# Sample attention of a hybrid decoder step: key tiles of a step made first, then mask, four logits matmuls and the value matmuls in chains

## The chip, the cores and the metric

One core of a Trainium2 chip runs the kernel. The metric is the device time of one launch in microseconds (us); the kernel before has a median of 2633.11 us over 3 runs (2631.79 to 2635.52).

## What is computed

The kernel is one inference step of a decoder layer: half an FFN, a mixer, half an FFN and a last norm, on 256 prompt rows and 64 sample rows (8 sequences of 8 new tokens). The mixer has a sparse attention (8 query heads, 2 key heads of 128) and a state-space part. The change lies in the attention of the sample rows over a paged cache of 2048 past keys for each sequence:

```python
score = jnp.where(admissible[None], score, -jnp.inf)
_, idx = lax.top_k(score, top)                       # 256 keys per query
k_sel, v_sel = gather_kv(idx)                        # pages of the cache
logits = jnp.einsum('bqkgd,bqskd->bqkgs', qg, k_sel) * HEAD_DIM ** -0.5
logits = jnp.where(valid, logits + bias, -jnp.inf)
p = jax.nn.softmax(logits, axis=-1)
out = jnp.einsum('bqkgs,bqskd->bqkgd', p, v_sel)
```

The kernel doesn't gather keys. It computes the logits of all 2112 keys and adds a mask of a large negative number where a key was not selected.

## The kernel before

Weights stream through SBUF in chunks of 512 KB (`chunk`, L147): a DMA fills `raw`, ScalarE rounds it to `hi` (L152), VectorE makes `lo = raw - hi` (L153), and TensorE takes three matmuls of 320 columns for each 128x128 piece (`mm3`, L163 to L165). Nearly all of TensorE's time is such matmuls.

The order of the instructions on each engine is made by a scheduler from the program's data dependencies and a cost model of its own. Only SP's queue is in the order in which the program is written, in the stage of the change (`manual_schedule(engines={SPE})`). TensorE takes its instructions strictly in the order made. So the matmuls of the sample attention stand among those of projections that have nothing to do with it (the input projection, `project`, and until about 1275 us the heads of the prompt attention), wherever the scheduler thought that their inputs would be there.

The sample attention works on pairs of sequences, i = 0 to 3, and on blocks of 512 keys, kb = 0 to 3: 16 steps. `logits_part(i, kb)` makes one step's logits:

- for each sequence of the pair, `kn` takes four pages of keys (four DMAs of 128 KB on SP, two buffers); eight transposes on TensorE (L136, `pe_t`) put the two key heads into two PSUM tiles, and ScalarE (L1072) and VectorE (L1070) copy these to two tiles `kt`. A step has four `kt`, q = 0 to 3, one for each sequence and key head;
- four logits matmuls (L1076) multiply the 32 query columns of `qS` with one `kt` each. The 32 columns of q go to the PSUM partitions 32q to 32q+31 of one tile `lg`, so each matmul uses 32 of the array's 128 columns, and the four use different ones;
- the mask is a matmul of `Rep` with `mkS` (L1077), over all 128 columns, into the same `lg`; then ScalarE copies `lg` to `pr` (L1078). The step with kb = 3 has a second, short group for the 64 new keys (L1084, L1085), and then the softmax.

`sample_pT` transposes the probabilities of a pair (17 transposes). `out_part(i - 1, kb)` multiplies them with the values one pair later: for each sequence, `vn` takes four pages of values (four buffers; the first sequence's pages by an indirect DMA of POOL, L1120, the second's by DMAs of SP, L1118; for i = 3 both by SP); then 16 matmuls (L1124), four pages by q = 0 to 3, again 32 columns each, q by q in different columns, all into one PSUM tile `po`. With kb = 3 come four more (L1129) for the new keys. The loop at the end of the stage calls `logits_part(i, kb)` and then `out_part(i - 1, kb)`.

A matmul of f32 data by f32 weights is two instructions in the trace, so the 64 logits matmuls appear as 128 and the 256 value matmuls as 512. Transposes and the matmuls of L163 to L165 are one each.

Of the kernel before, what the change touches and what calls it, by code (L numbers as in the profile page):

```python
# [10 lines left out]
F32 = mybir.dt.float32  # L11
# [10 lines left out]
P = 128  # L22
D = 2048
KT = D // P
TP = 256
NB = 8
NS = 8
TS = NB * NS
# [60 lines left out]
def tile_kernel(tc, I, O, ffn=True):  # L89
# [14 lines left out]
    def nm(s):  # L104
        uid[0] += 1
        return f"{s}_{uid[0]}"
# [7 lines left out]
    def pa_():  # L114
        return psA.tile([P, 512], F32, tag="a", name=nm("pa"))

    flip = [0]
# [297 lines left out]

    # ------------------------------------------------------------------ mixer
    Wi = I["w_in"][0]
# [96 lines left out]

    # ---- indexer
    qp = tc.alloc_tile_pool(name="qp", bufs=1)
# [52 lines left out]

    # dt, decays  # L570
    def sm(tag):
# [245 lines left out]

    # ---- prompt attention
    for h in range(NH):
# [33 lines left out]

    # ---- SSD
    cn = pa.tile([P, 12, 27], F32, tag="cn", name="cn", bufs=1)
# [194 lines left out]

    # ---- sample attention
    cv = I["cache_v"][0].rearrange("n k v d -> (n k) (v d)")
# [4 lines left out]

    def logits_part(i, kb, pr_, mx):
        kts = []
        for bb in range(2):  # L1060
            kn = sa.tile([P, 4, 256], F32, tag="kn", name=nm("kn"), bufs=2)
            for g, src in enumerate(pages(I["cache_k"], 2 * i + bb, 4 * kb, 4)):
                SY.dma_start(kn[:, g, :], src)
            for kv in range(2):
                pt = pa_()
                for g in range(4):
                    pe_t(pt[:, g * P:(g + 1) * P], kn[:, g, kv * P:(kv + 1) * P])
                kt = sa.tile([P, 512], F32, tag="kt", name=nm("kt"), bufs=4)
                if kv:
                    V.tensor_copy(kt, pt)  # L1070
                else:
                    S.copy(kt, pt)  # L1072
                kts.append(kt)
        lg = pa_()
        for q in range(4):
            TE.matmul(lg[32 * q:32 * q + 32], qs(i, q), kts[q], start=True, stop=False)  # L1076
        TE.matmul(lg, Rep[:, kb // 2, i, :], mkS[:, 512 * (kb % 2):512 * (kb % 2) + 512], start=False, stop=True)  # L1077
        S.copy(pr_[:, 512 * kb:512 * kb + 512], lg)  # L1078
        if kb < 3:
            V.tensor_reduce(mx[:, kb:kb + 1], pr_[:, 512 * kb:512 * kb + 512], axis=AX.X, op=ALU.max)  # L1080
            return
        lg = pa_()
        for q in range(4):
            TE.matmul(lg[32 * q:32 * q + 32, :TS], qs(i, q), kT[:, q % 2, TP:T], start=True, stop=False)  # L1084
        TE.matmul(lg[:, :TS], Rep[:, 1, i, :], mkS[:, PAST // 2:HK], start=False, stop=True)  # L1085
# [6 lines left out]
        V.tensor_scalar(pr_, pr_, mx[:, 6:7], None, op0=ALU.mult)  # L1092

    def sample_pT(pr_):
# [14 lines left out]

    def out_part(i, kb, pT, po):  # L1110
        vns = []
        for bb in range(2):
            vn = sa.tile([P, 4, 256], F32, tag="vn", name=nm("vn"), bufs=4)
            on_sp = pages(I["cache_v"], 2 * i + bb, 4 * kb, 4) if bb or i == 3 else None
            for g in range(4):
                pg_i = (2 * i + bb) * NPG + 4 * kb + g
                if on_sp is not None:
                    SY.dma_start(vn[:, g, :], on_sp[g])  # L1118
                else:
                    G.indirect_dma_start(out=vn[:, g, :], out_offset=None, in_=cv, in_offset=bass.IndirectOffsetOnAxis(ap=pti[:, pg_i:pg_i + 1], axis=0))  # L1120
            vns.append(vn)
        for g in range(4):
            for q in range(4):
                TE.matmul(po[32 * q:32 * q + 32, :P], pT[:, 4 * kb + g, 32 * q:32 * q + 32], vns[q // 2][:, g, (q % 2) * P:(q % 2 + 1) * P],  # L1124
                          start=(kb == 0 and g == 0), stop=False)
        if kb < 3:
            return
        for q in range(4):
            TE.matmul(po[32 * q:32 * q + 32, :P], pT[:TS, 16, 32 * q:32 * q + 32], vnat[:TS, 2, (q % 2) * P:(q % 2 + 1) * P], start=False, stop=True)  # L1129
        osb = sa.tile([P, 512], F32, tag="kt", name=nm("osb"), bufs=4)[:, 0:P]  # L1130
        S.copy(osb, po[:, :P])
# [7 lines left out]
    for i in range(5):  # L1139
# [65 lines left out]

    # ---- output projection
    Wo = I["w_out"][0]
# [105 lines left out]
```

## Time and profile before

| what | value |
|---|---|
| median of 3 runs | 2633.11 us (2631.79 to 2635.52) |
| span of the profiled execution (the page gives no other time of it) | 2630.1 us |
| TensorE busy, share of the span | 2581.9 us, 98% |
| chain that ended last: share of TensorE | 89% |
| mean granted TensorE clock | 0.994 |
| stage of the sample attention, first logits matmul to the point where both orders are the same again | 1221.8 to 1468.0 us |
| in that stage: DMA engines' busy share, bytes per second | 0.65, 197 GB/s |
| in that stage: VectorE and ScalarE busy | 112.6 and 105.0 of 246.2 us |

How to read it: a page gives one execution by the hardware's profiler. PE is TensorE's matmuls, PEld its weight loads, DVE is VectorE, ACT ScalarE, POOL GpSimd, and SPq the queue of SyncE, which issues most DMAs. In a timeline row, the first number is the start and the second the duration; consecutive matmuls of one form are one row with their count behind x. Matmuls are pipelined: one that has just started lets the next start before its end, so what a matmul costs is the distance from its start to the start of the next, and not its duration. Matmuls in different columns of the array can run beside each other, and their rows then overlap.

### The profile page before, as it was taken

What the parts mean: (1) busy time and instruction counts of PE and PEld (TensorE: products, weight loads), DVE (VectorE), ACT (ScalarE), POOL (GpSimd) and SP (SyncE); (2) the same over time, 40 slices, a digit from 0 to 9 for tenths busy, and PEclk for the clock granted to TensorE, in tenths of its full rate; (3) what the DMA queues carried; (4) which work ended last, traced back from release to release, by engine and by line L of the source; (5) the groups of instructions that cost most, each with busy time, mean ns of one, the idle gap of its engine ahead of it and who ended that gap; (6) DMA issues with size and microseconds to landing.
All of it is one profiled execution on the core that took longest, in us unless ns stands there. A gap on an engine that the chain in (4) does not pass through costs nothing.

```text
span 2630.1 us, 43071 instructions
## 1 busy us (share of the span) xinstructions
PE 2581.9 (98%) x17617; PEld 2446.9 (93%) x17617; DVE 1333.8 (51%) x2052; ACT 1042.2 (40%) x1446; POOL 180.4 (7%) x243
## 2 busy tenths in 40 slices
PE   8999999999999999999999999999999999999997
PEld 7999999999999998787676878999999999999997
DVE  6444444444444556686444466644444444444444
ACT  5333333333333443675443444533333333333333
POOL 3000000000000020000331121200000000000001
PEclk9999999999999999999999999999999999999999
DMA  6444444444454454245666544444444444444443
GB/s 204 145 146 151 152 147 150 153 148 150 142 159 148 156 165 144 76 122 170 186 198 210 174 141 151 137 150 148 152 152 146 152 152 146 151 144 155 151 137 120
DMA packets 401282, 399.70 MB, mean 152 GB/s; under 512 B 22344, under 2 KB 395949, under 8 KB 400572
## 3 DMA queue, kind: packets, MB, share of 16 engines
q1 hardware_dynamic: 366380, 358.76, 44.0%
q10 hardware_dynamic: 30800, 26.23, 3.4%
q0 software_dynamic: 3904, 11.96, 1.4%
q8 instruction: 138, 2.26, 0.3%
q14 instruction: 60, 0.49, 0.1%
HBM read 386.00 MB, written 10.88 MB: 151 GB/s over the span
## 4 chain that ended last, share of the span: by engine, by line
PE 89%; DVE 4%; DMA 2%; ACT 1%; issue 1%; SPq 0%; POOL 0%; ACTq 0%; DVEq 0%; POOLq 0%
PE pw L164 10%; PE pw L163 10%; PE pw L165 9%; PE pa L164 9%; PE pa L163 9%; PE pa L165 9%; PE pm L163 9%; PE pm L164 9%; PE pm L165 9%; PE pa L1076 2%; PE pa L136 1%; DVE lo L153 1%; PE pm L136 1%; PE pm L1124 1%; PE pa L677 1%
## 5 line engine op out<-in xcount | busy, mean ns | idle before, releaser
L153 DVE TENSOR_TENSOR lo<-raw,hi 128x1024 fp32r<-128x1024 f32 (+1 forms) x659 | 798.1, 1213 | 882.6 <-ACT hi L152 873.8
L152 ACT CAST hi<-raw 128x1024 fp32r<-128x1024 f32 (+1 forms) x659 | 676.1, 1026 | 1084.1 <-PE pm L164 439.7
L163 PE MATMUL pw<-xh,hi 128*128 128x320 f32 x1360 | 427.0, 314 | 3.7 <-ACT hi L152 1.7
L165 PE MATMUL pw<-xh,lo 128*128 128x320 f32 x1360 | 424.8, 312 | 2.3 <-DVE lo L153 2.3
L164 PE MATMUL pw<-xl,hi 128*128 128x320 f32 x1360 | 425.2, 313 | 0.7 <-DVE xl L188 0.7
L163 PE MATMUL pa<-xh,hi 128*128 128x320 f32 x1056 | 326.5, 309 | 0.3 <-ACT hi L152 0.3
L165 PE MATMUL pa<-xh,lo 128*128 128x320 f32 x1056 | 326.2, 309 | 0.0
L165 PE MATMUL pm<-xh,lo 128*128 128x320 f32 x1056 | 326.2, 309 | 0.0
L164 PE MATMUL pa<-xl,hi 128*128 128x320 f32 x1056 | 326.1, 309 | 0.0
L163 PE MATMUL pm<-xh,hi 128*128 128x320 f32 x1056 | 325.9, 309 | 0.0
L164 PE MATMUL pm<-xl,hi 128*128 128x320 f32 x1056 | 325.8, 308 | 0.0
L163 PEld LDWEIGHTS pw<-xh,hi 128*128 128x128 f32 x1360 | 256.6, 189 | 12.8 <-issue 10.4
L165 PEld LDWEIGHTS pw<-xh,lo 128*128 128x128 f32 x1360 | 256.2, 188 | 12.0 <-issue 9.3
L164 PEld LDWEIGHTS pw<-xl,hi 128*128 128x128 f32 x1360 | 256.3, 188 | 10.9 <-issue 9.3
L163 PEld LDWEIGHTS pa<-xh,hi 128*128 128x128 f32 x1056 | 198.6, 188 | 0.7 <-ACT hi L152 0.4
L165 PEld LDWEIGHTS pa<-xh,lo 128*128 128x128 f32 x1056 | 198.6, 188 | 0.2
L165 PEld LDWEIGHTS pm<-xh,lo 128*128 128x128 f32 x1056 | 198.5, 188 | 0.3
L164 PEld LDWEIGHTS pa<-xl,hi 128*128 128x128 f32 x1056 | 198.6, 188 | 0.1
L163 PEld LDWEIGHTS pm<-xh,hi 128*128 128x128 f32 x1056 | 198.5, 188 | 0.1
L164 PEld LDWEIGHTS pm<-xl,hi 128*128 128x128 f32 x1056 | 198.5, 188 | 0.0
L197 POOL TENSOR_TENSOR acc<-acc,sq 128x320 f32<-128x320 f32 x55 | 60.3, 1096 | 1864.7 <-ACT sq L195 1863.8
L163 PE MATMUL pm<-hh,hi 128*128 128x320 f32 x528 | 162.9, 308 | 0.0
(445 smaller groups left out, 4014.2 us busy)
## 6 DMA issues: line engine op xcount, KB each, us to landing
raw<-in_w_ffn_dram SPq DMA_DIRECT2D x511, 512.0 KB
raw<-in_w_in_dram SPq DMA_DIRECT2D x40, 512.0 KB
raw<-in_w_in_dram ACTq DMA_DIRECT2D x40, 512.0 KB
kn<-in_cache_k_dram SPq DMA_DIRECT2D x128, 128.0 KB
raw<-in_w_out_dram SPq DMA_DIRECT2D x32, 512.0 KB
vn<-in_cache_v_dram SPq DMA_DIRECT2D x80, 128.0 KB
raw<-in_w_ffn_dram SPq DMA_DIRECT2D x34, 256.0 KB
hn<-in_state_ssm_dram SPq DMA_DIRECT2D x16, 256.0 KB
```

Source lines behind the costliest of these rows:

```text
L136: TE.transpose(out, in_, cst[:n, C_ID:C_ID + n])
L152: S.copy(hi, raw)
L153: V.tensor_sub(lo, raw, hi.bitcast(F32))
L163: TE.matmul(out, wh, xh, start=start, stop=False)
L164: TE.matmul(out, wh, xl, start=False, stop=False)
L165: TE.matmul(out, wl, xh, start=False, stop=stop)
L197: (V if k == KT - 1 else G).tensor_add(accs[0], accs[0], sq)
L677: TE.matmul(pr[:, bh * 256:(bh + 1) * 256], qq[:, b].rearrange("p h t -> p (h t)"), kk[:, :, :, b * NPG:(b + 1) * NPG], start=st, stop=not st)
L1076: TE.matmul(lg[32 * q:32 * q + 32], qs(i, q), kts[q], start=True, stop=False)
L1124: TE.matmul(po[32 * q:32 * q + 32, :P], pT[:, 4 * kb + g, 32 * q:32 * q + 32], vns[q // 2][:, g, (q % 2) * P:(q % 2 + 1) * P], start=(kb = ...
```

## The change

- `logits_part` is cut in two. `load_k` loads the pages and makes all four `kt` of the step; the new `logits_part` gets them. The loop calls `load_k(i, kb)`, `load_v(i - 1, kb)` (the loads of the former `out_part`), then `logits_part`, then `out_part`.
- The mask matmul comes first in its PSUM group (`start=True`) and the four logits matmuls after it (`start=False, stop=True`).
- A new helper, `block`, adds dependencies by hand: the first of the four logits matmuls depends on all four copies to `kt`, and each of the four on the one before it. The same for the value matmuls: the first of 16 (20 with kb = 3) depends on all eight loads of the step's pages, each on the one before it, and the first also on the last logits matmul of the step. The dependencies between matmuls set only the order on TensorE; those on copies and loads are waits.
- The pool of `kt` has 5 buffers in place of 4.

Ten lines are added above the stage, so L136 becomes L146, L163 to L165 become L173 to L175, L1076 becomes L1086, L1077 L1085, L1084 L1094, L1124 L1136, L1129 L1139.

```diff
+    def block(mms, inputs):
+        for m in inputs:
+            tc.add_manual_dep(mms[0].ins, m.ins.name, SYNC, reason="block inputs")
+        for a, b in zip(mms, mms[1:]):
+            tc.add_manual_dep(b.ins, a.ins.name, NOSYNC, reason="block order")
...
-                kt = sa.tile([P, 512], F32, tag="kt", name=nm("kt"), bufs=4)
-                if kv:
-                    V.tensor_copy(kt, pt)
-                else:
-                    S.copy(kt, pt)
+                kt = sa.tile([P, 512], F32, tag="kt", name=nm("kt"), bufs=5)
+                made.append(V.tensor_copy(kt, pt) if kv else S.copy(kt, pt))
                 kts.append(kt)
+        return kts, made
+
+    def logits_part(i, kb, pr_, mx, kts, made):
         lg = pa_()
-        for q in range(4):
-            TE.matmul(lg[32 * q:32 * q + 32], qs(i, q), kts[q], start=True, stop=False)
-        TE.matmul(lg, Rep[:, kb // 2, i, :], mkS[:, 512 * (kb % 2):512 * (kb % 2) + 512], start=False, stop=True)
+        TE.matmul(lg, Rep[:, kb // 2, i, :], mkS[:, 512 * (kb % 2):512 * (kb % 2) + 512], start=True, stop=False)
+        mms = [TE.matmul(lg[32 * q:32 * q + 32], qs(i, q), kts[q], start=False, stop=True) for q in range(4)]
+        block(mms, made)
...
-    def out_part(i, kb, pT, po):
-        vns = []
+    def load_v(i, kb):
+        vns, made = [], []
...
+    def out_part(i, kb, pT, po, vns, made, before):
+        mms = [TE.matmul(po[32 * q:32 * q + 32, :P], pT[:, 4 * kb + g, 32 * q:32 * q + 32], vns[q // 2][:, g, (q % 2) * P:(q % 2 + 1) * P],
+                         start=(kb == 0 and g == 0), stop=False) for g in range(4) for q in range(4)]
...
+        block(mms, made)
+        if before:
+            block(before[-1:] + mms[:1], [])
...
         for kb in range(4):
+            mms = None
             if i < 4:
-                logits_part(i, kb, pr_, mx)
+                kts, made = load_k(i, kb)
             if i > 0:
-                out_part(i - 1, kb, pT, po)
+                vns, vmade = load_v(i - 1, kb)
+            if i < 4:
+                mms = logits_part(i, kb, pr_, mx, kts, made)
+            if i > 0:
+                out_part(i - 1, kb, pT, po, vns, vmade, mms)
```

How this moves TensorE's instructions, at three places. In the rows, L163 to L165 (L173 to L175) are matmuls of a projection, `pa_` and `pm_` are PSUM tiles, and the number behind a tile's name tells one buffer from another.

TensorE before, the step i = 1, kb = 2, the four logits matmuls of `pa_12296`:

```order
L1076 MATMUL pa_12296<-kt_12259,qS 32x512
L136 MATMUL pa_12282<-cst,kn_12268 128x128 x2
L136 MATMUL pa_12289<-cst,kn_12268 128x128 x2
L1076 MATMUL pa_12296<-kt_12266,qS 32x512
L165 MATMUL pw_13875<-xh_8346,lo_13969 128x320
L163 MATMUL pw_14024<-xh_8345,hi_14028 128x320
L164 MATMUL pw_14024<-xl_8347,hi_14028 128x320
L1076 MATMUL pa_12296<-kt_12287,qS 32x512
```

The same step after the change:

```order
L173 MATMUL pw_14025<-xh_8345,hi_14058 128x320
L1086 MATMUL pa_12315<-kt_12259,qS 32x512
L1086 MATMUL pa_12315<-kt_12266,qS 32x512
L1086 MATMUL pa_12315<-kt_12287,qS 32x512
L1086 MATMUL pa_12315<-kt_12294,qS 32x512
L174 MATMUL pw_14025<-xl_8347,hi_14058 128x320
```

Before, each of the four stands alone between matmuls that use all 128 columns; after, the four stand in a row, and the mask's matmul has moved ahead of them.

TensorE before, value matmuls of the same step:

```order
L1124 MATMUL pm_12041<-vn_12309,pT_12011 32x128 x2
L1124 MATMUL pm_12041<-vn_12304,pT_12011 32x128 x2
L163 MATMUL pw_14024<-xh_8345,hi_14028 128x320
L1124 MATMUL pm_12041<-vn_12309,pT_12011 32x128 x2
L1124 MATMUL pm_12041<-vn_12304,pT_12011 32x128 x2
L164 MATMUL pw_14024<-xl_8347,hi_14028 128x320
```

And after:

```order
L175 MATMUL pw_14024<-xh_8346,lo_14089 128x320
L1136 MATMUL pm_12041<-vn_12296,pT_12011 32x128 x2
L1136 MATMUL pm_12041<-vn_12301,pT_12011 32x128 x2
...
L1136 MATMUL pm_12041<-vn_12296,pT_12011 32x128 x2
L1136 MATMUL pm_12041<-vn_12301,pT_12011 32x128 x2
L173 MATMUL pw_14024<-xh_8346,hi_14088 128x320
```

Before, a page's four value matmuls stand together, with a projection's matmul between pages; after, all 16 stand in a row.

TensorE after, the step i = 2, kb = 0: the last transposes of the first key buffer (`kn_12491`) and the first of the load that takes its place (`kn_12590`):

```order
L146 MATMUL pa_12512<-cst,kn_12491 128x128 x4
L146 MATMUL pa_12533<-cst,kn_12519 128x128 x4
L146 MATMUL pa_12540<-cst,kn_12519 128x128 x4
L1085 LDWEIGHTS Rep
L1085 MATMUL pa_12566<-mkS,Rep 128x512
L174 MATMUL pw_14175<-xl_8347,hi_14208 128x320
...
L174 MATMUL pw_14174<-xl_8348,hi_14238 128x320
L146 MATMUL pa_12604<-cst,kn_12590 128x128
L1086 MATMUL pa_12566<-kt_12510,qS 32x512
```

Between the two stand eight transposes, the mask and eight projection matmuls; a transpose of the new load stands ahead of the step's logits.

Over the whole stage, TensorE's order before has the 352 matmuls of 32 columns (64 + 16 of logits, 256 + 16 of values) in 101 unbroken runs; after, the same matmuls stand in 30 runs. The runs that hold logits matmuls of 512 keys are 48 before and 18 after; those that hold value matmuls are 53 and 16. Before, 60 runs are followed by a projection's matmul; after, 19. SP's order differs only in where three loads of the prompt attention stand. POOL keeps its instructions, some gathers of values a few places earlier or later; ScalarE has two loads of a function table more (32 for 30).

## Rows read from the trace of the kernel before

**Rows 1.** The page: busy time by engine, and the chain that ended last

```profile
PE 2581.9 (98%) x17617; PEld 2446.9 (93%) x17617; DVE 1333.8 (51%) x2052; ACT 1042.2 (40%) x1446; POOL 180.4 (7%) x243
...
PE 89%; DVE 4%; DMA 2%; ACT 1%; issue 1%; SPq 0%; POOL 0%; ACTq 0%; DVEq 0%; POOLq 0%
```

**Rows 2.** Windows: length, busy PE, PEld, DVE, ACT, POOL, clock, DMA share, GB/s

```profile
1441.50:1443.90 2.40, 0.35 (x5) 0.12 (x4) 0.00 (x0) 0.44 (x2) 2.04 (x4) 1.00 0.89 284
1443.90:1447.40 3.50, 3.50 (x17) 2.90 (x18) 0.00 (x0) 0.00 (x0) 0.08 (x1) 0.51 0.80 244
...
1221.80:1468.00 246.20, 241.63 (x1789) 166.59 (x1789) 112.61 (x192) 105.00 (x178) 59.58 (x88) 0.99 0.65 197
```

**Rows 3.** Timeline of PE, a logits matmul alone between others

```profile
1224.83 0.31 PE L163 MATMUL pw<-xh,hi 128*128 128x320 f32 x1
1224.98 0.30 PE L164 MATMUL pw<-xl,hi 128*128 128x320 f32 x1
1225.21 1.04 PE L1076 MATMUL pa<-kt,qS 128*32 128x512 f32 x2
1226.19 0.33 PE L136 MATMUL pa<-cst,kn 128*128 128x128 f32 x1
```

**Rows 4.** Timeline of PE, two, three and four logits matmuls in a row

```profile
1221.84 1.05 PE L1076 MATMUL pa<-kt,qS 128*32 128x512 f32 x4
1222.82 0.41 PE L165 MATMUL pw<-xh,lo 128*128 128x320 f32 x1
...
1244.08 1.06 PE L1076 MATMUL pa<-kt,qS 128*32 128x512 f32 x6
1245.07 0.39 PE L1077 MATMUL pa<-mkS,Rep 128*128 128x512 bf16 x1
...
1273.15 1.90 PE L1076 MATMUL pa<-kt,qS 128*32 128x512 f32 x8
1274.99 0.39 PE L1077 MATMUL pa<-mkS,Rep 128*128 128x512 bf16 x1
```

**Rows 5.** Timeline of PE, value matmuls of one page, and of eight

```profile
1285.24 0.43 PE L1124 MATMUL pm<-vn,pT 128*32 128x128 f32 x8
1285.60 0.42 PE L163 MATMUL pw<-xh,hi 128*128 128x320 f32 x1
1285.85 0.31 PE L164 MATMUL pw<-xl,hi 128*128 128x320 f32 x1
...
1438.67 1.96 PE L1124 MATMUL pm<-vn,pT 128*32 128x128 f32 x64
1440.55 0.84 PE L136 MATMUL pm<-cst,cn 128*27 128x128 f32 x6
```

**Rows 6.** Instructions of tiles kt and vn: count, duration ns min/median/max, first and last start

```profile
L1072 ACT COPY kt<-pa x32: 572/586/611, 1218.1 to 1419.8; 128x512 f32<-128x512 f32 x32
L1070 DVE COPY kt<-pa x32: 681/691/692, 1220.0 to 1420.0; 128x512 f32<-128x512 f32 x32
...
L1120 POOL DMA_INDIRECT vn<-in_cache_v_dram,pti x48: 942/949/1992, 1211.1 to 1409.8; - x48
...
DMA to landing us min/median/max: 4.6/4.9/5.9
```

**Rows 7.** Timeline of PE, key transposes of two loads of one buffer

```profile
1325.55 1.53 PE L136 MATMUL pa<-cst,kn 128*128 128x128 f32 x12
...
1329.94 0.66 PE L136 MATMUL pa<-cst,kn 128*128 128x128 f32 x4
```

**Rows 8.** Chain of waits from 1244 to 1250 us, a load of keys

```profile
1244.59 5.02 DMA kn<-in_cache_k_dram
```

**Rows 9.** Who PE waited for, 1220 to 1480 us: total, times, longest

```profile
PE pm L1124 <- DMA vn<-in_cache_v_dram: 2.0, 1, 2.0
PE pa L136 <- DMA kn<-in_cache_k_dram: 2.0, 2, 1.7
PE pa L136 <- issue: 0.4, 1, 0.4
PE pa L136 <- DVE pr L1092: 0.2, 1, 0.2
```

**Rows 10.** Who SP's queue waited for, 1220 to 1470 us

```profile
SPq L1063 <- PE pa L136: 36.2, 11, 10.1
SPq L1063 <- DMA raw<-in_w_in_dram: 20.9, 7, 5.6
SPq L1118 <- DMA raw<-in_w_in_dram: 13.8, 3, 5.8
```

More of the change, by code (lines that the diff above doesn't have):

```diff
@@ L115, in pa_ @@
         return psA.tile([P, 512], F32, tag="a", name=nm("pa"))
+    SYNC = mybir.DependencyInfo(mybir.DependencyClass.Sync, mybir.DependencyReason.DATA)
+    NOSYNC = mybir.DependencyInfo(mybir.DependencyClass.NoSync, mybir.DependencyReason.DATA)
+    def block(mms, inputs):
[3 more added lines that the diff above has]
+            tc.add_manual_dep(b.ins, a.ins.name, NOSYNC, reason="block order")
     flip = [0]
@@ L1056, in qs, with load_k @@
         return qS[:, 2 * i + q // 2, 4 * (q % 2):4 * (q % 2) + 4, :].rearrange("p g t -> p (g t)")
-    def logits_part(i, kb, pr_, mx):
-        kts = []
+    def load_k(i, kb):
+        kts, made = [], []
         for bb in range(2):
@@ L1080, in logits_part @@
             V.tensor_reduce(mx[:, kb:kb + 1], pr_[:, 512 * kb:512 * kb + 512], axis=AX.X, op=ALU.max)
-            return
+            return mms
         lg = pa_()
-        for q in range(4):
-            TE.matmul(lg[32 * q:32 * q + 32, :TS], qs(i, q), kT[:, q % 2, TP:T], start=True, stop=False)
-        TE.matmul(lg[:, :TS], Rep[:, 1, i, :], mkS[:, PAST // 2:HK], start=False, stop=True)
+        TE.matmul(lg[:, :TS], Rep[:, 1, i, :], mkS[:, PAST // 2:HK], start=True, stop=False)
+        last = [TE.matmul(lg[32 * q:32 * q + 32, :TS], qs(i, q), kT[:, q % 2, TP:T], start=False, stop=True) for q in range(4)]
+        block(mms[-1:] + last, [])
         S.copy(pr_[:, PAST:SK], lg[:, :TS])
@@ L1092, in logits_part @@
         V.tensor_scalar(pr_, pr_, mx[:, 6:7], None, op0=ALU.mult)
+        return mms + last
     def sample_pT(pr_):
@@ L1117, in out_part @@
                 if on_sp is not None:
-                    SY.dma_start(vn[:, g, :], on_sp[g])
+                    made.append(SY.dma_start(vn[:, g, :], on_sp[g]))
                 else:
-                    G.indirect_dma_start(out=vn[:, g, :], out_offset=None, in_=cv, in_offset=bass.IndirectOffsetOnAxis(ap=pti[:, pg_i:pg_i + 1], axis=0))
+                    made.append(G.indirect_dma_start(out=vn[:, g, :], out_offset=None, in_=cv, in_offset=bass.IndirectOffsetOnAxis(ap=pti[:, pg_i:pg_i + 1], axis=0)))
             vns.append(vn)
[L1122 to L1125, printed above, removed]
+        return vns, made
+    def out_part(i, kb, pT, po, vns, made, before):
+        mms = [TE.matmul(po[32 * q:32 * q + 32, :P], pT[:, 4 * kb + g, 32 * q:32 * q + 32], vns[q // 2][:, g, (q % 2) * P:(q % 2 + 1) * P],
+                         start=(kb == 0 and g == 0), stop=False) for g in range(4) for q in range(4)]
+        if kb == 3:
+            mms += [TE.matmul(po[32 * q:32 * q + 32, :P], pT[:TS, 16, 32 * q:32 * q + 32], vnat[:TS, 2, (q % 2) * P:(q % 2 + 1) * P],
+                              start=False, stop=True) for q in range(4)]
+        block(mms, made)
+        if before:
+            block(before[-1:] + mms[:1], [])
         if kb < 3:
             return
-        for q in range(4):
-            TE.matmul(po[32 * q:32 * q + 32, :P], pT[:TS, 16, 32 * q:32 * q + 32], vnat[:TS, 2, (q % 2) * P:(q % 2 + 1) * P], start=False, stop=True)
-        osb = sa.tile([P, 512], F32, tag="kt", name=nm("osb"), bufs=4)[:, 0:P]
+        osb = sa.tile([P, 512], F32, tag="kt", name=nm("osb"), bufs=5)[:, 0:P]
         S.copy(osb, po[:, :P])
```

## The prediction

> **What bounds the kernel now.** I read the page first: TensorE is busy for 98% of the span and makes 89% of the chain that ended last [rows 1]. So what counts is how long TensorE takes for its instructions in their order; work of another engine counts only where TensorE waits for it. The windows come next: from the first logits matmul to the point where both orders are the same again the stage takes 246 us, at full clock but for one piece, with DMA engines 65% busy and VectorE and ScalarE under half [rows 2]. The list of waits says that TensorE stands still in the stage for under 5 us in all: once 2.0 us for a page of values, twice for keys (2.0 us), and two short ones [rows 9]. So the stage is bound by TensorE's stream, and its price is read from the timeline, as distances from start to start.
>
> The timeline shows what the change is about. A projection's matmul is followed by the next after 0.15 us. A logits matmul alone (two records, 32 of 128 columns) holds the stream for 0.98 us, 1225.21 to 1226.19, and starts 0.23 us after its forerunner, not 0.15 [rows 3]. Two in a row take 0.98 us as well, and three 0.99: they run beside each other in their own columns [rows 4]. Four in a row are in the trace too, with 1.84 us; but there the fourth has to wait until VectorE's copy of its `kt` is done, so this is 0.99 and a wait of 0.85 [rows 4]. The value matmuls show that four different column groups do run together: a set of four (eight records) takes 0.36 us, and 32 of them in a row 1.88, so each further set costs (1.88 - 0.36) / 7 = 0.22 [rows 5].
>
> **The change part by part.** The median of the runs is 2633.1 us, the profiled span 2630.1; the 3.0 us outside are launch and end, which nothing here touches. Gains go from both alike.
>
> *Logits.* The order has 48 runs that hold logits matmuls before and 18 after. A run costs about 0.98 us whether it holds one matmul or four. 30 fewer by 0.98 is **29.4 us**.
>
> *Values.* 53 runs before, 16 after. A set of four that joins a run costs 0.22 in place of 0.36: 37 by 0.14 is **5.2 us**.
>
> *Entering and leaving.* Each of the 101 runs is entered with 0.23 - 0.15, about 0.09 us, more than the step to an ordinary neighbour [rows 3]; 71 fewer is **6.4 us**. Leaving to a projection costs as much again: the matmul after a value run is followed by the next after 0.25 us, not 0.15 [rows 5]. 60 such exits before, 19 after: 41 by 0.10 is **4.1 us**.
>
> Sum: 45 us. Going through all neighbours of the stage one by one, with the distance that each kind of pair has in the trace, gives more: 239 us for the order before, without waits (measured 246), and 187 for the one after, 52 less. The rest is in sets of values that were cut in half, and in the waits of a fourth logits matmul. I take 48, with 45 and 52 as its ends.
>
> *Moved for nothing.* The mask's matmul stands ahead of the four instead of behind them: same instruction, same length; `lg` is held no longer than before. The fifth `kt` buffer costs space only. ScalarE's two further table loads lie beside TensorE; ScalarE is busy for 105 of 246 us [rows 2], so there is room unless a copy queues behind one. SP issues the same DMAs in the same order.
>
> *New waits.* They take a part of it back, since all loads and copies keep their length while TensorE needs 48 us less for the stage. Four kinds:
>
> - Keys. A `kn` buffer can be filled only after its last transpose. In the trace the next load's first transpose follows 4.0 us after it without a wait (the row of twelve begins with the last four of the old load, to 1325.98; the next begin at 1329.94) [rows 7]; a load on the chain took 5.0 [rows 8]. In the third order piece above only eight transposes (0.9 us), the mask (0.2) and eight projection matmuls (1.2) lie between, 2.3 us: a wait of 1.7 to 2.7. I count three such places (i = 0, 2 and 3) and two of about 1 us in i = 1: 7 to 10, I take 8.5.
> - Copies. The head of each of the 16 blocks now waits for all four copies. After the last transpose lie 1.1 to 2.2 us of other work; the copy takes 0.69 on VectorE or 0.59 on ScalarE [rows 6], if the engine is free. Between 0 and the 0.85 of the trace's four in a row, I take 0.3 each: 5 us.
> - Pages of values. The first of 16 waits for all eight pages. Between nothing and, in each of the 12 later steps, the 2.0 of the one wait seen [rows 9], 24 us. I take 3, nearer to the rows: in 16 steps there was one.
> - The rest (softmax, half clock): after the wait of 2.05 us at 1441.5 the granted clock was 0.51 of full speed, the lower level of 1.2 GHz, for some 3.4 us [rows 2], 1.7 us lost; one more of these, and 2 us of the softmax: 3.5.
>
> That is 20 us of waits, where before had 4.6 [rows 9], three times 0.85 in fourth logits matmuls, and the 1.7 of half clock, 8.9 together. Net 11 to 12. So 48 - 12 = **36 us less: 2597 us**. What is late next is the load of keys: SP's queue already waits for TensorE to free a buffer most of all, and for chunks of weights to land, 20.9 and 13.8 us in ten waits [rows 10].
>
> After the stage TensorE goes on with the same projections as before, 36 us earlier; their weights come through ScalarE's queue, ahead by as much. I see nothing that gives the gain back there.
>
> The trace has three logits matmuls in the time of one, 2.95 times as fast as three alone [rows 4]. The Trainium skill, page "TensorE: Matmul & The Clock Gate", section "Part 3: Packing small matmuls — row/col tiling", has 2.38 for three column tiles of 512 columns; by it, as an estimate, four would be 3.2 times as fast, a block 1.23 us in place of 1.0, and 16 blocks 4 us less gain, 2601. The trace decides here, as the rows are of these very matmuls.
>
> **The rivals.**
>
> *All of the gain stays.* Loads and copies are in time, and no wait is longer than before: 52 less, 2581. For it: DMA engines are 65% busy, and the scheduler has put the blocks behind other work. Against: the third order piece, where 2.3 us stand against a load of at least 4.0.
>
> *The loads set the pace.* With 246 - 48 us for the same bytes the DMA share rises from 0.65 to 0.81 on average [rows 2], and SP's waits for weight chunks, up to 5.8 us each [rows 10], are no longer covered. If five to six of the ten such waits reach TensorE by 3 us, 16 us more go: 20 left, 2613. For it: those waits are there. Against: TensorE noticed hardly any of them, and of a step's 14 us some 11 remain.
>
> *Slower: the head of the value chain.* Before, TensorE could take one page's matmuls as soon as that page was there; now nothing behind the block goes on until all eight have landed, four of them gathers that POOL issues in 0.95 us each and that land 4.9 later [rows 6], 8.7 us after POOL is free. If POOL is held by the convolution's copies, each of the 12 blocks fed by it can wait. From 48 / 12 = 4 us each the gain is gone; at 5 us, 60 us of waits, 12 us slower: 2645. Against: four value buffers, two steps ahead, and one wait of 2.0 so far.
>
> *Four don't run together.* If the fourth column group, or the dependencies by hand, made the four go one after the other, a block would take 3.9 us and the logits would gain nothing but the entries: about 16 us for values and switches, less 12 of waits, 2629. Against: sets of four values in 0.36 us [rows 5].
>
> **How the numbers follow.** My forecast, with waits of 14 to 30 us, 2590 to 2607: 0.58. All of the gain: 0.18. Loads set the pace: 0.18. Slower: 0.03. Not together: 0.03. A measurement of this kernel can tell about 0.2%, 5 us, from no change. Faster by more than that are the first three and a third of the last, 0.95; within it 0.02; slower 0.03. The range reaches from the full gain to the paced stage and a little beyond each, 2580 to 2617.
>
> **What would show it.** In the profile after: 16 or so groups of eight logits records, each some 1.0 us from start to the next start; value groups of 32 records with 1.0 us; the stage's projections as dense as before; TensorE's waits in the stage at some 20 us, most of them for `kn` at kb = 1 of a pair. Right, if the stage is about 210 us long and everything after it as long as before. Wrong, if the four are 0.9 us apart each (no overlap), if waits for `vn` lead the list with more than 20 us (the slower rival), or if projections after the stage wait for weights.

## The result and the profile after

The changed kernel takes **2591.3 us** (median of four runs, 2589.9 to 2595.4), the kernel before 2633.8 beside it (2631.8 to 2635.5): 42.6 us less, a ratio of 0.9844 with a 95% interval of 0.9832 to 0.9855. The profiled execution went from 2630.1 to 2590.2 us of span.

First the page of the changed kernel, busy time and the chain that ended last, to be read against [rows 1]:

```profile
PE 2534.6 (98%) x17617; PEld 2442.9 (94%) x17617; DVE 1332.2 (51%) x2052; ACT 1044.0 (40%) x1448; POOL 176.9 (7%) x243
...
PE 88%; DVE 4%; DMA 2%; ACT 1%; issue 1%; SPq 1%; POOL 0%; ACTq 0%; DVEq 0%; POOLq 0%
```

TensorE has the same number of matmuls, 17617, and is busy 47.3 us less. The other engines do what they did. The windows (length, busy PE, PEld, DVE, ACT, POOL, granted clock, DMA share, GB/s) say where: ahead of the stage, in it, and behind the point where both orders are the same again.

```profile
0.00:1221.80 1221.80, 1199.32 (x8071) 1164.90 (x8072) 641.96 (x1105) 503.64 (x688) 57.32 (x95) 0.99 0.48 148
...
1221.80:1428.43 206.63, 195.79 (x1799) 164.44 (x1797) 111.96 (x193) 108.56 (x179) 55.88 (x88) 0.98 0.76 231
1428.43:2590.20 1161.77, 1139.48 (x7752) 1113.51 (x7750) 578.25 (x755) 431.81 (x581) 63.65 (x60) 1.00 0.47 148
```

The first matmul that stands elsewhere in the order starts at 1223.1 (the mask's), before at 1221.8 (a logits matmul); from there to the place where the orders are the same again the stage lasted 205.3 us, before 246.1, from 1221.84 to 1467.98. What follows takes 1161.8 us, before 2630.1 - 1468.0 = 1162.1. So the whole gain is made inside the stage and nothing is given back behind it.

Groups of instructions of TensorE in the stage, the kernel before (line, names, shapes, count, busy us, mean ns, idle time ahead of them):

```profile
L1076 PE MATMUL pa<-kt,qS 128*32 128x512 f32 x128 | 53.1, 604 | 0.0
...
L1124 PE MATMUL pm<-vn,pT 128*32 128x128 f32 x512 | 27.4, 282 | 2.0 <-DMA vn<-in_cache_v_dram 2.0
```

And the changed kernel:

```profile
L146 PE MATMUL pa<-cst,kn 128*128 128x128 f32 x246 | 42.4, 282 | 6.4 <-DMA kn<-in_cache_k_dram 6.0
L1086 PE MATMUL pa<-kt,qS 128*32 128x512 f32 x128 | 19.1, 604 | 0.0
L1136 PE MATMUL pm<-vn,pT 128*32 128x128 f32 x512 | 17.2, 275 | 4.5 <-DMA vn<-in_cache_v_dram 3.9 <-issue 0.5
```

The mean length of one matmul is as it was (604 ns). Only the time in which any of them runs has shrunk, because more of them run at once: logits 53.1 to 19.1 us, values 27.4 to 17.2. The timeline of the changed kernel shows what one chain looks like (start, length):

```profile
1336.11 0.30 PE L174 MATMUL pw<-xl,hi 128*128 128x320 f32 x1
1336.34 1.07 PE L1086 MATMUL pa<-kt,qS 128*32 128x512 f32 x8
1337.34 0.42 PE L175 MATMUL pw<-xh,lo 128*128 128x320 f32 x1
...
1353.03 1.07 PE L1086 MATMUL pa<-kt,qS 128*32 128x512 f32 x8
1353.92 0.29 PE L1094 MATMUL pa<-kT,qS 128*32 128x64 f32 x8
1354.03 1.06 PE L1136 MATMUL pm<-vn,pT 128*32 128x128 f32 x32
1355.01 0.42 PE L1139 MATMUL pm<-vnat,pT 64*32 64x128 f32 x8
```

Four logits matmuls (eight records) from 1336.34 to the next start at 1337.34 hold the stream for 1.00 us, as long as one alone did [rows 3]; sixteen value matmuls (32 records) hold it for 0.98. Two of the sixteen logits chains, the first and the fourth, were cut by three transposes of the prompt attention; the rest look like this.

The waits of TensorE from 1220 to 1440 us, the answer to [rows 9]:

```profile
PE pa L146 <- DMA kn<-in_cache_k_dram: 6.0, 5, 2.8
PE pm L1136 <- DMA vn<-in_cache_v_dram: 3.9, 4, 1.4
PE pm L1136 <- issue: 0.5, 2, 0.4
```

10.4 us, before 4.6. The longest is worth a look. The chain of waits around it (start, length, what):

```profile
1336.41 1.04 PE pa L1086 x8
1337.45 0.19 SPq L1073
...
1337.84 5.84 DMA kn<-in_cache_k_dram
...
1343.72 0.69 PE pa L146 x2
```

And the windows of that wait and behind it:

```profile
1340.50:1343.60 3.10, 0.42 (x4) 0.19 (x2) 0.00 (x0) 0.56 (x2) 2.08 (x5) 0.87 1.03 335
...
1342.80:1343.70 0.90, 0.00 (x0) 0.00 (x0) 0.00 (x0) 0.00 (x0) 0.90 (x1) 0.51 0.92 247
1343.70:1349.70 6.00, 5.97 (x24) 5.59 (x25) 1.92 (x2) 1.53 (x2) 1.93 (x3) 0.50 0.87 275
1349.70:1353.00 3.30, 3.30 (x25) 3.07 (x23) 0.69 (x1) 1.16 (x2) 0.00 (x0) 1.00 0.58 167
```

A load of keys took 5.84 us while the DMA engines were full (share 1.03 as the view counts it, 335 GB/s). TensorE stood still for 2.8 us, and when it went on the granted clock was 0.50 of full speed, the lower level of 1.2 GHz, for 6.0 us more: 3.0 us of work lost. (The clock was at 0.51 for the last 0.9 us of the wait too, where there was nothing to lose.) So this one late load cost 2.8 us directly and about as much again through the clock.

Why was it late? The eight transposes that read its buffer last were done at 1331.8 (the last two start from 1331.41), but the load went out only at 1337.84. In between SP stood at a load of values ahead of it in its queue. From SP's list of waits, 1330 to 1345 us:

```profile
SPq L1129 <- DMA raw<-in_w_in_dram: 4.5, 1, 4.5
```

So most of this delay is SP's queue, held by what the list puts down to a chunk of weights, and not the buffer.

### The profile page after: what moved, and what is told of

Its sections match the earlier page's. It is cut to its first block, busy times and chain, and to the rows that moved or that the text cites. A ratio compares the mean times of both kernels' runs of the same rounds, so it can differ in the third digit from the quotient of the medians.

```text
span 2590.2 us, 43131 instructions
## 1 busy us (share of the span) xinstructions
PE 2534.6 (98%) x17617; PEld 2442.9 (94%) x17617; DVE 1332.2 (51%) x2052; ACT 1044.0 (40%) x1448; POOL 176.9 (7%) x243
## 4 chain that ended last, share of the span: by engine, by line
PE 88%; DVE 4%; DMA 2%; ACT 1%; issue 1%; SPq 1%; POOL 0%; ACTq 0%; DVEq 0%; POOLq 0%
PE pw L173 10%; PE pw L174 9%; PE pw L175 9%; PE pa L173 9%; PE pa L174 9%; PE pm L173 9%; PE pa L175 9%; PE pm L175 9%; PE pm L174 9%; DVE lo L163 1%; PE pa L146 1%; PE pm L146 1%; PE pa L687 1%; DMA kn<-in_cache_k_dram 1%; DMA raw<-in_w_in_dram 1%
## 5 line engine op out<-in xcount | busy, mean ns | idle before, releaser
L163 DVE TENSOR_TENSOR lo<-raw,hi 128x1024 fp32r<-128x1024 f32 (+1 forms) x659 | 798.2, 1214 | 868.9 <-ACT hi L162 862.0
L173 PE MATMUL pw<-xh,hi 128*128 128x320 f32 x1360 | 427.6, 314 | 4.2 <-ACT hi L162 1.6
L175 PE MATMUL pw<-xh,lo 128*128 128x320 f32 x1360 | 424.9, 313 | 2.3 <-DVE lo L163 2.3
L173 PE MATMUL pa<-xh,hi 128*128 128x320 f32 x1056 | 326.5, 309 | 0.3 <-ACT hi L162 0.3
L175 PE MATMUL pa<-xh,lo 128*128 128x320 f32 x1056 | 326.3, 309 | 0.0
L175 PE MATMUL pm<-xh,lo 128*128 128x320 f32 x1056 | 326.2, 309 | 0.0
L173 PE MATMUL pm<-xh,hi 128*128 128x320 f32 x1056 | 326.0, 309 | 0.0
L173 PEld LDWEIGHTS pw<-xh,hi 128*128 128x128 f32 x1360 | 256.9, 189 | 10.4 <-issue 7.1
L175 PEld LDWEIGHTS pw<-xh,lo 128*128 128x128 f32 x1360 | 256.9, 189 | 4.7 <-DVE lo L163 2.5
L173 PEld LDWEIGHTS pa<-xh,hi 128*128 128x128 f32 x1056 | 198.5, 188 | 0.7 <-ACT hi L162 0.4
L175 PEld LDWEIGHTS pa<-xh,lo 128*128 128x128 f32 x1056 | 198.6, 188 | 0.2
L175 PEld LDWEIGHTS pm<-xh,lo 128*128 128x128 f32 x1056 | 198.5, 188 | 0.3
L173 PEld LDWEIGHTS pm<-xh,hi 128*128 128x128 f32 x1056 | 198.6, 188 | 0.1
L173 PE MATMUL pm<-hh,hi 128*128 128x320 f32 x528 | 162.9, 308 | 0.0
```

Source lines behind the costliest of these rows:

```text
L163: V.tensor_sub(lo, raw, hi.bitcast(F32))
L173: TE.matmul(out, wh, xh, start=start, stop=False)
L175: TE.matmul(out, wl, xh, start=False, stop=stop)
```

## The experiments

The theory: the gain is the number of unbroken runs of small matmuls, since those in different column groups then run beside each other; the price is the waits at the heads. The rivals: the loads and buffers that were rearranged make the gain; a fixed order would be enough; it is standing in a row that helps, not the columns.

**Logits chains alone.** The value chains are taken out, and with them their place behind the last logits matmul.

```diff
-        block(mms, made)
-        if before:
-            block(before[-1:] + mms[:1], [])
```

(in `out_part`)

> The chains of the value matmuls are taken out, those of the logits stay. The order of this kernel has 18 runs of logits (as the changed kernel) and about 30 of values (16). My theory: the time of the stage is the sum of the distances between neighbours plus waits, and most of the gain is in the logits. By the distances measured before, this order is 5.5 us longer than the changed one without waits, and a chain that waits for all eight pages is gone, so some 2 to 3 us of waits for vn go: 2594 us, 2590 to 2599. A rival, that half or more of the gain is in the value chains (fewer cuts, fewer changes of the tile shape), gives 2605 or more.

Measured: 2597.7 us (2594.5 to 2603.0), ratio 0.9870 [0.9854, 0.9887]. Within the range expected: 36 of the 42.6 us are there without the value chains. One part fell: the waits for values did not shrink (3.3 and 1.7 us in its list of waits), and copies of key tiles were now waited for (3.8 us).

**Value chains alone.** The chains of the logits go, with the one that held the short group for the 64 new keys behind them, and the values no longer stand behind the last logits matmul; the mask stays ahead of the four.

```diff
-        block(mms, made)
...
-        block(mms[-1:] + last, [])
...
-                out_part(i - 1, kb, pT, po, vns, vmade, mms)
+                out_part(i - 1, kb, pT, po, vns, vmade, None)
```

> The chains of the logits are taken out, those of the values stay, and so does the mask ahead of the four. The order has some 45 runs with logits and 19 with values. My theory: logits cut apart cost about 0.98 us for each run again; by distances this order is 34 us longer than the changed one, and a stage that is longer waits less for keys, by up to 10 us: 2616 us, 2608 to 2626, so most of the gain is gone. The rival that the gain comes from where the loads and copies stand, not from the chain of four, gives 2591 to 2597.

Measured: 2618.7 us (2617.8 to 2620.6), ratio 0.9946 [0.9929, 0.9962], as expected. Its stage, groups of TensorE's instructions:

```profile
L1086 PE MATMUL pa<-kt,qS 128*32 128x512 f32 x128 | 49.1, 604 | 0.0
...
L1134 PE MATMUL pm<-vn,pT 128*32 128x128 f32 x512 | 18.7, 276 | 1.4 <-DMA vn<-in_cache_v_dram 0.9 <-issue 0.5
```

The values have nearly the changed kernel's 17.2, the logits nearly the 53.1 of before.

**No chain.** Every call of `block` goes; early key tiles, early value loads, mask first and the fifth key tile stay.

> No chain at all; what stays of the change is that a step's key tiles are made first, its value loads stand ahead of the logits, the mask comes first and there is a fifth key tile. The order has some 41 runs of logits and 51 of values. My theory: by distances 40 us longer than the changed kernel, 11 us shorter than the kernel before, with some 10 us fewer waits than the changed kernel: 2622 us, 2614 to 2632. The rival that the loads and buffers make the gain: 2591 to 2600.

Measured: 2633.5 us (ten runs, 2628.4 to 2634.7), ratio 0.9995 [0.9986, 1.0005]: no change from the kernel before. The rival that loads and buffers make the gain has fallen. My own number fell too, 11 us too low. I had expected the waits to shrink; its trace has these from 1218 to 1475 us, 10.0 us together, 0.9 of them just ahead of the stage:

```profile
PE pm L1134 <- issue: 3.1, 1, 3.1
PE pa L146 <- DMA kn<-in_cache_k_dram: 2.4, 4, 1.2
PE pm L1134 <- DMA vn<-in_cache_v_dram: 2.3, 1, 2.3
PE pm L1134 <- DMA vn<-in_cache_v_dram,pti: 1.9, 1, 1.9
PE pa L146 <- ACT kt L1079: 0.3, 1, 0.3
```

**One column group for the logits.**

```diff
-        mms = [TE.matmul(lg[32 * q:32 * q + 32], qs(i, q), kts[q], start=False, stop=True) for q in range(4)]
+        mms = [TE.matmul(lg[0:32], qs(i, q), kts[q], start=(q == 0), stop=(q == 3)) for q in range(4)]
```

(The mask's matmul stays, as a group of its own with `stop=True`.)

> All four logits matmuls of a chain write the same 32 rows of their PSUM tile, and so use the same 32 columns of the array; the logits of three of the four and the mask are not what the reference has. Chains, loads, copies and the rest stay. My theory: the four of a chain run beside each other only because they use four different column groups; in one column group each takes its 0.9 to 1.0 us, a chain 3.6 to 3.9 in place of 1.0, 16 chains 42 to 46 us more, of which the shorter waits for keys and pages give back up to 10: 2628 us, 2622 to 2640. The rival that the gain is only in standing in a row (no change of tile shape between neighbours), whatever the columns: 2591 to 2596.

**One column group for the values**, the same for the sixteen (and the four with `kb` = 3):

```diff
-        mms = [TE.matmul(po[32 * q:32 * q + 32, :P], pT[:, 4 * kb + g, 32 * q:32 * q + 32], vns[q // 2][:, g, (q % 2) * P:(q % 2 + 1) * P],
+        mms = [TE.matmul(po[0:32, :P], pT[:, 4 * kb + g, 32 * q:32 * q + 32], vns[q // 2][:, g, (q % 2) * P:(q % 2 + 1) * P],
...
```

> All sixteen value matmuls of a chain write the same 32 rows of their PSUM tile, so use the same 32 columns of the array; VectorE writes zeros to the tile first. The attention outputs of the samples are thus sums over four heads groups in one place and zeros in the others. Chains, loads and copies stay. My theory: a matmul of 128 columns in two passes takes 0.22 us by itself, and sets of four take 0.22 only because the column groups work side by side; a chain of sixteen is then 3.5 to 3.7 us in place of 1.0, sixteen chains 40 to 43 us more, of which shorter waits give back some 10, as they did for the logits: 2622 us, 2614 to 2634. The rival that standing in a row without a change of tile shape is what helps: 2590 to 2596.

Measured: logits in one group 2622.7 us (2620.9 to 2624.7), ratio 0.9958 [0.9942, 0.9975]; values in one group 2630.6 us (2627.3 to 2636.8), ratio 0.9994 [0.9984, 1.0003]; both lie within the ranges expected. The logits in the stage of the one, and one of its chains:

```profile
L1086 PE MATMUL pa<-kt,qS 128*32 128x512 f32 x128 | 59.2, 596 | 0.7 <-DVE kt L1079 0.7
```

```profile
1307.30 3.19 PE L1086 MATMUL pa<-kt,qS 128*32 128x512 f32 x7
...
1310.33 0.59 PE L1086 MATMUL pa<-kt,qS 128*32 128x512 f32 x1
...
1310.77 0.31 PE L1136 MATMUL pm<-vn,pT 128*32 128x128 f32 x3
```

And a chain of the other:

```profile
1316.33 1.07 PE L1086 MATMUL pa<-kt,qS 128*32 128x512 f32 x8
1317.21 3.66 PE L1136 MATMUL pm<-vn,pT 128*32 128x128 f32 x32
1320.80 0.88 PE L146 MATMUL pa<-cst,kn 128*128 128x128 f32 x6
```

Each matmul is as long as before. The second kernel has the chains of the changed one (18 runs with logits, 15 with values); in the first the four logits chains of i = 0 were cut (23 runs with logits), the other twelve stand whole. But its logits are now busy 59.2 us in place of 19.1, and a whole chain holds the stream for 3.5 us (1307.30 to 1310.77) in place of 1.0; sixteen values hold it for 3.6 us (1317.21 to 1320.80) in place of 0.98. So it is the four column groups beside each other that make a chain short, by 3.5 and 3.7 times. The rival of standing in a row has fallen. That the logits' total grew by 31.5 and not by the 40.1 of busy time is in part less waiting (7.6 us in its list against 10.4) and in part the 3.0 us lost at half clock, of which this run has none; the values' total grew by 39.3, where I had counted on 10 us fewer waits and its waits stayed at some 10.

**The order without the waits.** `block` keeps the dependencies from one matmul to the next and loses those of the head on the inputs.

```diff
-        for m in inputs:
-            tc.add_manual_dep(mms[0].ins, m.ins.name, SYNC, reason="block inputs")
```

> The chains keep their order, one matmul after the other, but their head no longer has to wait for all inputs of the chain: each matmul waits for its own input alone, as it did before the change. The order then has about 70 runs with sample matmuls, 45 with logits and 34 with values. My theory: a run stays whole only because its first matmul waits for everything that the others need, so that nothing else is put between; without that the order is by distances 37 us longer than the changed one. The kernel with no chains came out 42 us above the changed one, so: 2626 us, 2616 to 2632. The rival that the fixed order is enough gives 2590 to 2596.

Measured: 2615.3 us (2614.1 to 2617.3), ratio 0.9930 [0.9915, 0.9945]: 24 us above the changed kernel and just below the range expected. The logits in its stage, and then its waits there:

```profile
L1084 PE MATMUL pa<-kt,qS 128*32 128x512 f32 x128 | 49.6, 604 | 0.0
```

```profile
PE pa L144 <- DMA kn<-in_cache_k_dram: 1.1, 2, 0.7
PE pm L1134 <- DMA vn<-in_cache_v_dram: 0.2, 1, 0.2
```

A fixed order is not enough: other matmuls stand between the four again (45 runs with logits in its trace), presumably because the scheduler fills the time in which inputs of the later ones are on their way, and the logits are back at 49.6 us. It came out 11 us better than I expected; this order hardly waits, 1.3 us in all.

**The sum over these kernels.** For each, the order's price without waits (all neighbours of the stage by the distances of the trace, as in the prediction), the waits that TensorE's list shows in the stage, and both together and the time as differences from the changed kernel:

| kernel | logits / value runs | order, us | waits, us | both | measured |
|---|---|---|---|---|---|
| changed | 18 / 16 | 187.0 | 10.4 | 0 | 0 |
| logits chains alone | 18 / 30 | 192.5 | 11.7 | +6.8 | +6.4 |
| order without waits | 45 / 34 | 224.2 | 1.3 | +28.1 | +24.0 |
| value chains alone | 45 / 19 | 221.1 | 5.0 | +28.7 | +27.5 |
| no chain | 41 / 51 | 227.6 | 10.0 | +40.2 | +42.3 |
| before | 48 / 53 | 238.8 | 4.6 | +46.0 | +42.6 |

The order's price was known ahead of the runs, the waits were read behind them. With both, no kernel is off by more than about 4 us from the medians. But the waits come from single executions, so the stages of the same executions are the fairer comparison: between the same two places of the order they are 3.0, 24, 27, 38 and 40.8 us longer than the changed kernel's, down the table; the sum is above all five, by 2 to 5. A part of that is the half clock, which the table leaves out: it cost the changed kernel 3.0 us, value chains alone and the kernel before 1.7 each, no chain 3.4, and the other two nothing. With it the sums are +3.8, +25.1, +27.4, +40.6 and +44.7.

**What the waits are worth.** Keys loaded in the first step only, and read again in all later ones:

```diff
+            if i == 0 and kb == 0:
+                kn = sa.tile([P, 4, 256], F32, tag="kn", name=nm("kn"), bufs=2)
...
+                kept.append(kn)
+            kn = kept[bb]
```

> The keys are loaded for the first step alone, and the transposes of all later steps read these two buffers again; the logits of the other steps are thus of other keys than the reference's. Transposes, copies and chains stay. My theory: the waits for keys (6.0 us), the half clock after the longest (over 1 us) and most of the waits for values go, since half of the stage's bytes are gone, and the order is 2 us shorter by distances: 2580 us, 2575 to 2586. The rival that the waits for loads cost the stage nothing, because TensorE would be held by the next thing at the same place: 2588 to 2592.

Measured: 2581.1 us (2580.2 to 2582.5), ratio 0.9803 [0.9788, 0.9818]: 10.1 us below the changed kernel. What TensorE still waits for in the stage is 3.9 us ahead of values, put down to issue. By distances its order is 2.3 us shorter than the changed one. Of the other 7.8 us, all waits of its stage give 5.4 (10.4 to 5.0: the 3.9, and two of 0.7 and 0.4 behind the chains) and the half clock 1.3: it did not go, as I had expected, but fell from 3.0 to 1.7 us, now behind one of the waits for values.

**Finer key buffers.** One page each, ten with four key tiles, or eight with five:

```diff
-            kn = sa.tile([P, 4, 256], F32, tag="kn", name=nm("kn"), bufs=2)
+            kns = []
...
+                kns.append(sa.tile([P, 256], F32, tag="kn", name=nm("kn"), bufs=10))
+                SY.dma_start(kns[g], src)
...
-                kt = sa.tile([P, 512], F32, tag="kt", name=nm("kt"), bufs=5)
+                kt = sa.tile([P, 512], F32, tag="kt", name=nm("kt"), bufs=4)
```

> The keys are loaded into ten buffers of one page each, in place of two buffers of four pages, and the key tiles go back from five to four to pay for it. A page's buffer comes free after its own two transposes, and two pages more are in flight. My theory: the changed kernel waits 6.0 us in five places for keys whose load could not start before the last of eight transposes, and loses over 1 us of clock after the longest; half to two thirds of it goes: 2587 us, 2583 to 2592. The rival that these loads are late because the DMA engines are full (share 0.76 in the stage) and not for a buffer gives 2590 to 2593; a rival that the fifth key tile is what lets the chains stand gives over 2594.

> The keys are loaded into eight buffers of one page each (the same bytes as the two of four pages), and the five key tiles stay. My theory: a page's load can start as soon as its own two transposes are done, some 0.1 to 0.4 us earlier than with a whole buffer, so of the 6.0 us of waits for keys 1 to 2 go: 2590 us, 2586 to 2593. The rival that the buffers set nothing: 2591.

Measured: ten pages 2586.7 us (2584.4 to 2592.4), ratio 0.9826 [0.9813, 0.9840]; eight pages 2593.0 us (2590.9 to 2598.4), ratio 0.9852 [0.9839, 0.9866]. The waits of the kernel with ten, and of that with eight:

```profile
PE pa L146 <- DMA kn<-in_cache_k_dram: 4.5, 3, 2.7
PE pm L1137 <- DMA vn<-in_cache_v_dram: 3.3, 2, 2.0
```

```profile
PE pa L146 <- DMA kn<-in_cache_k_dram: 10.2, 8, 3.2
...
PE pm L1137 <- DMA vn<-in_cache_v_dram: 0.2, 1, 0.2
```

Eight pages hold the same bytes as before, and nothing is gained: the wait for values moved to the keys. With ten the clock stays at 1.00 in every part of the stage, also around its wait of 2.7 us, which is nearly as long as the one of 2.8 in the changed kernel that was followed by half clock:

```profile
1340.00:1380.00 40.00, 35.26 (x364) 28.86 (x363) 22.82 (x40) 18.91 (x32) 20.06 (x24) 1.00 0.85 267
```

So what it has less of is 2.6 us of waits and 3.0 us of half clock. Its median is the lowest of the kernels that leave nothing out, 4.6 us under the changed one, but the two intervals overlap, so it isn't shown to be faster.

**Four key tiles, and page buffers for the values.** The changed kernel with `bufs=4` for `kt` alone; then twelve key pages, fourteen one-page value buffers and four key tiles; then ten, fourteen and five.

```diff
-            vn = sa.tile([P, 4, 256], F32, tag="vn", name=nm("vn"), bufs=4)
+            vn = [sa.tile([P, 256], F32, tag="vn", name=nm("vn"), bufs=14) for g in range(4)]
```

> The changed kernel with four key tiles in place of five; the key loads stay in two buffers of four pages. My theory: a chain uses four key tiles and all are free again long before the next step's copies, so the fifth is worth nothing, and what the kernel with ten page buffers gained comes from its pages: 2591 us, 2588 to 2595. The rival that it is the number of key tiles (through the places where transposes and copies are put) that gave the gain: 2584 to 2588; a rival that the fifth tile is needed: over 2596.

> As the kernel with ten one-page key buffers and four key tiles, but with twelve key pages, and the values too in buffers of one page each, fourteen in place of four times four: the same bytes. My theory: that kernel still waits 4.5 us for keys and 3.3 us for values in the stage; two more key pages in flight and earlier freed value pages take up to half of it: 2584 us, 2580 to 2589. The rival that two value pages fewer make the values late, and what the keys gain is lost there: 2587 to 2594.

> Ten one-page buffers for the keys, fourteen for the values, and five key tiles: the bytes of the kernel with twelve, fourteen and four, with the fifth key tile back for two key pages. The trace of that one has waits of 7 us for the copies of key tiles, and the changed kernel with four key tiles has 5 us of them; the changed kernel with five has none. My theory: the fifth tile keeps the copies out of TensorE's way, and the pages keep the keys' waits at 2 to 5 us: 2588 us, 2583 to 2593. The rival that the loss of the kernel with twelve and fourteen came from the two value pages that it has fewer: 2597 to 2603.

Measured: four key tiles 2596.3 us (2594.5 to 2597.0), ratio 0.9863 [0.9846, 0.9879]; twelve, fourteen and four 2601.1 us (2598.6 to 2603.4), ratio 0.9879 [0.9863, 0.9896]; ten, fourteen and five 2607.2 us (2603.8 to 2607.7), ratio 0.9898 [0.9881, 0.9914]. None of my three numbers held: the first is just above 2595 and where the rival "the fifth tile is needed" begins (2596), the other two are far above their ranges. With four key tiles TensorE waits for copies of them, 4.9 us, where the changed kernel has no such wait:

```profile
PE pa L1086 <- DVE kt L1079: 2.9, 2, 1.7
...
PE pa L1093 <- ACT kt L1079: 2.0, 1, 2.0
```

From the lists of the last kernel, who TensorE and who POOL's gathers waited for:

```profile
PE pa L146 <- ACT kt L1080: 5.9, 2, 3.7
PE pm L1137 <- DMA vn<-in_cache_v_dram: 5.1, 3, 2.8
```

```profile
POOL vn L1132 <- PE pm L1137: 29.7, 7, 8.9
...
POOL vn L1132 <- PE pa L146: 1.8, 5, 0.5
```

And in the changed kernel:

```profile
POOL vn L1131 <- PE pa L146: 18.0, 3, 7.2
POOL vn L1131 <- PE pm L1136: 14.5, 3, 9.1
```

The gathers wait for TensorE about as long in both, 31.5 and 32.5 us, so a longer wait of POOL is not what makes the difference. TensorE's own waits do: 21.8 us in the stage in place of 10.4, 10.1 of them for copies of key tiles, and three stretches of 3.4 us at half clock, 5.1 us lost in place of 3.0. That is 13.5 of the 16 us. Copies are late in this kernel although it has five tiles, so the fifth tile alone doesn't keep them in time. What the two slow kernels share is the value buffers, 14.4 us slower than ten key pages with four tiles and 16.0 slower than the changed kernel: a loss larger than the rival said. But that change is two, two pages fewer and pages taken one by one, and no run takes them apart; why the copies come late was not traced either. The ten key pages are worth 9.6 us against the kernel with the same four key tiles (intervals 0.9813 to 0.9840 and 0.9846 to 0.9879 are apart). What the fifth tile is worth by itself, 5.1 us by the medians, is at the edge of what can be told (the intervals 0.9846 to 0.9879 and 0.9832 to 0.9855 overlap).

## Why the prediction was right, point by point

- **What bounds the stage: right.** TensorE's stream with its distances. The table above gives five other kernels by it to about 5 us.
- **Logits, 48 runs to 18, and a run as long with four as with one: right.** A chain holds the stream for 1.00 us where 0.98 was taken. The Trainium skill, page "TensorE: Matmul & The Clock Gate", section "Part 3: Packing small matmuls — row/col tiling", has 2.38 for three column tiles; by it, as an estimate, a block would have been 1.23 us. The trace doesn't agree here: 1.00, and the four in one group hold the stream 3.5 times as long, where the estimate had 3.2.
- **Sum of the gain: 48 taken, perhaps under-sized.** I took 48, between 45 from single terms and 52 from all neighbours. The sum over neighbours, 238.8 - 187.0 = 51.8, leaves 7.3 us for everything else in the stage before (246.1) and 18.3 after (205.3); 51.8 less the 11.0 between them is the measured 40.8. The traces show 13.4 of the 18.3, as said next, so a gain between 48 and 52 fits them, and not 45. The single terms left out sets of values that had been cut: values went down by 10.2 us of busy time, where my term had 5.2.
- **New waits, 20 us: total nearly right, its parts not.** The stage took 205.3 us against 187.0 without waits: 18.3. Waits are 10.4 of it and half clock 3.0. Keys: 8.5 taken, 6.0 measured, five waits as I had counted, but not all at kb = 1. At the place of the third order piece it was 1.22 us (1.7 to 2.7 expected); the longest, 2.8 at 1343.7, belongs to the last step of i = 2, where I had none, and came from SP's queue, not from the buffer that I had reasoned with. Copies: 5 taken, none in the list; that was the worst term: the 1.1 to 2.2 us of other work behind the last transpose were enough. Pages of values: 3 taken, 3.9 and 0.5. Softmax: 2 taken, none. Half clock: 1.7 taken, 3.0. 4.9 us are left over; the list doesn't say where, and a part may belong to the sum over neighbours. So it is luck that the total is near: copies and softmax, 7 us taken and none found, stand against these 4.9 and the longer half clock.
- **Net: 36 taken, 42.6 measured**, 2597 against 2591. In the profiled stage it is 40.8: by the sum over neighbours the gross was 4 too low and the net waits (12 taken, 11.0) 1 too high. If what is left over belongs to that sum, the gross of 48 was right, and the net waits were 7 in place of 12; the traces don't settle which. The rest between 40.8 and 42.6 is how single executions differ.
- **Moved for nothing: right but for one.** Mask, table loads and SP's order show nothing. Of the fifth `kt` buffer I said that it costs space only; without it the median is 5 us higher and TensorE waits 4.9 us for copies, though the intervals overlap.
- **Rivals.** "All of the gain stays" (2581) is what the kernel without key loads gives, 2581.1; the price of the key loads is that difference less the 2.3 us by which its order is shorter. "The loads set the pace": the DMA share rose to 0.76, not 0.81, and one load, held in SP's queue behind a wait put down to a weight chunk and then slow in full engines, cost 2.8 us and the clock. That is this rival's mechanism; it is real, but seen once and not five times. The head of the value chain: 3.9 us in four waits, nowhere near the 48 it needed. Four not together: no.

## What to carry to other kernels

Matmuls that use a quarter of the columns should stand in unbroken runs over all four column groups; here that was worth some 50 us of 246 before waits and 41 with them, and either kind of matmul forced into one group gave most of it back. With a scheduler, an order alone does not keep a run whole; the head must wait for the inputs of all. Then look at what the faster stage waits for: a late load can be paid twice, by the wait and by the clock behind it (2.8 and 3.0 us here, but a wait of 2.7 with ten key pages left the clock alone), and moving the buffers' bytes about can cost more than the wait was worth, as in the kernel with fourteen value pages, ten key pages and five key tiles (16 us).

## What the runs showed of the hardware

Sixteen value matmuls of 128 columns in four column groups take 0.98 us, in one group 3.6: nearly the full factor of four, also for runs this short. After TensorE stood still for 2.8 us the granted clock was 0.50 for 6.0 us; around waits of 1.2 and 1.4 us in the same stage, and of 2.7 us in the kernel with ten key pages, the means of the 40 to 48 us stayed at 1.00. So the length of a wait alone didn't tell whether the clock would fall. A load of keys took 5.84 us to land with the DMA engines full, where one on the chain of the kernel before took 5.02 [rows 8].

Left open: SP issues the loads of the next step's keys behind those of this step's values; the late load went out at 1337.8, after a load of values at 1336.4 that SP had stood at for 4.5 us. Whether keys issued ahead of the values would take the longest wait away was not tried.
